# At the end of each stage: the second tile's scaled rows ahead of all splits

## The chip, the core and the metric

The kernel runs on one core of a Trainium2 chip. The core has five engines that this text calls PE (TensorE, the matrix multiplier), DVE (VectorE), ACT (ScalarE), POOL (GpSimd) and SP (SyncE, which here issues the loads from memory). The metric is the device time of one execution in microseconds (us), less being better.

## What is computed

Two blocks on a batch of 256 tokens of width 1024, all in fp32. Cut to the order of the stages:

```python
# first block, i = 0 (mLSTM) and i = 1 (sgu)
h = rmsnorm(x, norm_g[i, 0]) * (1.0 + sc1) + sh1       # sc, sh, g: rows of silu(c) @ ada_w[i] + ada_b[i]
y = mlstm_mixer(h, ...) if i == 0 else sgu_mixer(h, ...)
x = x + g1 * rmsnorm(y, norm_g[i, 1])
h = rmsnorm(x, norm_g[i, 2]) * (1.0 + sc2) + sh2
y = square(relu(h @ ffn_w1[i])) @ ffn_w2[i]
x = x + g2 * rmsnorm(y, norm_g[i, 3])
# second block
h = rms_norm(x, attn_norm_g); proj = h @ w_in          # attention and convolution branches, gated
x = x + mixed @ w_out
h2 = rms_norm(x, ffn_norm_g); x = x + peer(h2, ...)    # experts picked by product keys
h3 = rms_norm(x, ple_norm_g)
x = x + sigmoid(h3 @ w_ple_gate) * (p @ w_ple_proj)
```

Each stage ends in the same way: a residual add, a norm over 1024 columns, a scale (and a shift), and the next stage's first matrix product.

## The kernel before

The 256 tokens are two tiles of 128. An fp32 product is made of three products of split operands: `split` (L351) writes `hi`, the operand cast to a shorter form (ACT, L352), and `lo`, the rest (DVE, L353); PE then adds hi·hi, lo·hi and hi·lo (L113, or L384 to L386 for transposed results). Weights arrive as `st` tiles of 128x2048 fp32 (1 MB), loaded by SP in program order (L358) into a pool of three buffers, `wst`; each is split in two halves, `hi`/`lo` of 128x1024. A buffer is free for the next load when the last reader of its tile is done. A scheduler lays down one fixed order of instructions on each engine; `behind()` (L294) adds a constraint: what is issued inside it stands behind the instructions `net.lo` (DVE) and `net.hi` (ACT) on their engines. The weights' splits use it too (L372), each behind the one before it.

The end of a stage is `Finish`. `chain(t)` makes the norm of tile t and its normed rows `xn` (DVE L191, ACT L192). `turn(t)` transposes `xn` in eight 128x128 pieces on PE (L203), four into the PSUM tile `sd` and four into `mm`; DVE scales and shifts the first four (L212), ACT the other four (L214, or L216 with a shift), into `hf`. `split(t)` makes `hhi` (ACT) and `hlo` (DVE) of these rows. `run(t)` is the head: the next stage's first columns, computed by PE in plain fp32 (L135) from the unsplit weights and from `hf`, so that PE has work while the splits are made. The head's weights are two or three `st` tiles, held until tile 1's head has read them. There are seven such ends: into the mLSTM (1), the first ffn (2), the sgu (3), the second ffn (4), the mixing stage of the second block (5), the experts (6) and the last stage (7, which has no head). Text and rows below use these numbers. The tiles of the rows and of the order: `ada` is an accumulator of the modulation rows on DVE, fed by `ada_w` loads; `b_w_v` and `b_w_u` are the sgu's weights, `ffn_w2` the second ffn's, `peer_q` the experts' queries'.

`end` (L229 to L243) is the place of the change: behind the `xn` rows (`self.at`) it issues tile 0's splits, then tile 1's `turn`, `run` and splits.

Of the kernel before, what the change touches and what calls it, by code (L numbers as in the profile page):

```python
# [16 lines left out]
AF = mybir.ActivationFunctionType  # L17
ALU = mybir.AluOpType
# [119 lines left out]
class Finish:  # L138
# [55 lines left out]
    def turn(self, t):  # L194

        net, nc = self.net, self.net.nc
        g, sh = self.g, self.sh
        pss = []
        for q in range(2):
            ps = (net.sd_tile, net.mm_tile)[q]().rearrange("p (k c) -> p k c", k=4)  # L200
            for k in range(4):
                kk = 4 * q + k
                nc.tensor.transpose(ps[:, k], self.xn[:, kk * 128:(kk + 1) * 128], net.ident)  # L203
            pss.append(ps)
        for q, ps in enumerate(pss):
            hf = self.room(512, 1024 * t + 512 * q, "hf", 4).rearrange("p (k c) -> p k c", k=4)
            self.hf[t, q] = hf
            for k in range(4):
                kk = 4 * q + k
                gk, sk = g[:, kk:kk + 1], None if sh is None else sh[:, kk:kk + 1]  # L210
                if q == 0:
                    nc.vector.tensor_scalar(hf[:, k], ps[:, k], gk, sk, op0=ALU.mult, op1=ALU.bypass if sh is None else ALU.add)  # L212
                elif sh is None:
                    nc.scalar.activation(hf[:, k], ps[:, k], AF.Copy, scale=gk)  # L214
                else:
                    nc.scalar.activation(hf[:, k], ps[:, k], AF.Identity, scale=gk, bias=sk)  # L216

    def split(self, t):
        for q in range(2):
# [8 lines left out]
    def end(self, acc, last=None):  # L228

        net = self.net  # L230
        if self.head is not None:
            net.head = Head(net, self.head, self.head_pool)
        self.chain(1, acc)
        self.run(0)

        net.lo, net.hi = self.at
        with net.behind():
            if self.head is not None:
                self.x = net.h_tiles()
                self.split(0)  # L240
            self.turn(1)
            self.run(1)
            self.split(1)  # L243

    def whole(self):
# [17 lines left out]
class Net:  # L263
# [613 lines left out]
    def mix(self, x):  # L877
        nc, a = self.nc, self.a
        with ExitStack() as es:
# [168 lines left out]
            def head(h):  # L1048
                pl = self.sd_tile()[:, :384]
                for t, s, w in segs:  # L1050
                    nc.tensor.matmul(pl[:, s], qn[:, h // 2, t * 128:(t + 1) * 128], kz[:, h, :w], start=True, stop=True)
                lg = p2.tile([128, 384], F32, tag="rl", name="lg")
                nc.vector.tensor_tensor(lg, pl, bm[:, h], op=ALU.add)
                mx = self.small.tile([128, 2], F32, tag="mx", name="mx")
                pr = p2.tile([128, 384], F32, tag="pr", name="pr")
                for t, s, w in segs:
                    nc.vector.tensor_reduce(mx[:, t:t + 1], lg[:, s], axis=AX.X, op=ALU.max, negate=True)
                    nc.scalar.activation(pr[:, s], lg[:, s], AF.Exp, bias=mx[:, t:t + 1], accum_out=rs[:, t, h:h + 1])

                def turn():  # L1060
                    pt = self.sd_tile()[:, :384]
                    for e in range(3):
                        b = slice(e * 128, (e + 1) * 128)
                        nc.tensor.transpose(pt[:, b], pr[:, b], self.ident)
                    pts = p2.tile([128, 384], F32, tag="pts", name="pts")
                    self.last = nc.scalar.copy(pts, pt)
                    self.defer(lambda: weigh(pts))

                def weigh(pts):
                    vs = slice(h * 64, (h + 1) * 64)  # L1070
                    nc.tensor.matmul(av[1][:, vs], pts[:, 0:128], v[:, 0, vs], start=True, stop=False)
                    nc.tensor.matmul(av[1][:, vs], pts[:, 128:256], v[:, 1, vs], start=False, stop=True)
                    nc.tensor.matmul(av[0][:, vs], pts[:, 256:384], v[:, 0, vs], start=True, stop=True)

                self.defer(turn)
# [432 lines left out]
```

## Time and profile before

| what | us |
|---|---|
| median of three runs (lowest, highest) | 1772.01 (1771.02, 1776.46) |
| the profiled execution | 1775.46 |
| its span from the first to the last instruction | 1773.8 |
| PE busy | 1719.7 (97%) |
| DVE busy | 1385.0 (78%) |
| ACT busy | 873.9 (49%) |

Each row of the timeline is an instruction, or several of one kind in a row (x4): its start, how long the group took, engine, line, what it writes and reads, and in brackets how long the engine had been idle before and what ended that. The mean granted clock of PE over the span was 0.994 of full speed.

### The profile page before, as it was taken

Reading aid. Unit: us, or ns where it says so; the run is one execution under the profiler, and the core shown is the slowest. Engines: PE = TensorE matmul, PEld = TensorE weight load, DVE = VectorE, ACT = ScalarE, POOL = GpSimd, SP = SyncE. Lnnn points to the kernel's source line nnn. Section 1 sums busy time; section 2 is a strip of 40 time slices with the busy share of each in tenths; the row PEclk is TensorE's granted clock in tenths of the full one; section 3 lists DMA queues with packets and bytes.
Section 4 is the critical chain, followed back from the end, with each engine's and each line's share of the span. In section 5 each row is a group of like instructions: output and inputs, shape, how many; then the busy total and the mean of one; then the engine's idle time right before and its main releaser. Section 6 shows DMA issues by size and latency. Waiting matters only on the chain.

```text
span 1773.8 us, 29281 instructions
## 1 busy us (share of the span) xinstructions
PE 1719.7 (97%) x11754; PEld 1537.7 (87%) x11754; DVE 1385.0 (78%) x2394; ACT 873.9 (49%) x1404; POOL 27.6 (2%) x42
## 2 busy tenths in 40 slices
PE   7998999999999999999899999999999999999998
PEld 3877899987889898889889999999988998787786
DVE  6687986578958555899757999789788948888754
ACT  3564555454545444565545445445444444455544
POOL 0010000000000000000000000000000000000000
PEclk9999999999999999999899999999999999999999
DMA  9875987376838552544426555544555455554751
GB/s 334 299 286 186 335 354 257 138 270 243 303 118 294 186 190 95 198 143 143 146 95 219 183 174 183 182 166 168 175 176 180 144 190 175 182 186 155 258 190 48
DMA packets 59603, 352.48 MB, mean 199 GB/s; under 512 B 6165, under 2 KB 12613, under 8 KB 19273
## 3 DMA queue, kind: packets, MB, share of 16 engines
q1 hardware_dynamic: 59466, 350.61, 56.3%
q8 instruction: 92, 1.51, 0.3%
q14 instruction: 45, 0.37, 0.1%
HBM read 349.51 MB, written 1.07 MB: 198 GB/s over the span
## 4 chain that ended last, share of the span: by engine, by line
PE 83%; DVE 8%; DMA 3%; ACT 3%; issue 2%; POOL 1%; SPq 0%; POOLq 0%; DVEq 0%; ACTq 0%
PE acc L113 37%; PE mm L384 13%; PE mm L386 13%; PE mm L385 13%; DVE lo L353 2%; PE head L135 2%; PE sd L1171 1%; PE sd L1182 1%; ACT hi L352 1%; DVE ada L509 1%; ACT junk L164 1%; DMA st<-in_a_w_v_dram 1%; PE sd L804 1%; DMA X<-in_x_dram 1%; POOL rs_r L429 0%
## 5 line engine op out<-in xcount | busy, mean ns | idle before, releaser
L352 ACT CAST hi<-st 128x1024 fp32r<-128x1024 f32 (+1 forms) x507 | 525.7, 1048 | 487.6 <-PE mm L385 234.8
L353 DVE TENSOR_TENSOR lo<-st,hi 128x1024 fp32r<-128x1024 f32 (+1 forms) x507 | 613.9, 1220 | 174.5 <-ACT hi L352 172.9
L384 PE MATMUL mm<-hhi,hi 128*128 128x256 f32 (+1 forms) x2000 | 574.0, 287 | 1.9 <-ACT hi L352 1.2
L386 PE MATMUL mm<-hhi,lo 128*128 128x256 f32 (+1 forms) x2000 | 566.5, 284 | 4.9 <-DVE lo L353 4.8
L385 PE MATMUL mm<-hlo,hi 128*128 128x256 f32 (+1 forms) x2000 | 566.7, 283 | 0.0
L386 PEld LDWEIGHTS mm<-hhi,lo 128*128 128x128 f32 (+1 forms) x2000 | 383.2, 192 | 5.8 <-DVE lo L353 5.7
L384 PEld LDWEIGHTS mm<-hhi,hi 128*128 128x128 f32 (+1 forms) x2000 | 383.5, 192 | 4.5 <-ACT hi L352 1.8
L385 PEld LDWEIGHTS mm<-hlo,hi 128*128 128x128 f32 (+1 forms) x2000 | 383.6, 192 | 2.2 <-issue 1.1
L113 PE MATMUL acc<-hi,vh 128*128 128x512 f32 x448 | 142.5, 399 | 0.9 <-ACT vh L352 0.9
L113 PE MATMUL acc<-lo,vh 128*128 128x512 f32 x448 | 138.8, 391 | 0.0
L113 PE MATMUL acc<-hi,vl 128*128 128x512 f32 x448 | 137.9, 389 | 0.0
L113 PE MATMUL acc<-hi,h 128*128 128x512 f32 x320 | 100.7, 394 | 0.0
L113 PEld LDWEIGHTS acc<-hi,vl 128*128 128x128 f32 x448 | 84.1, 188 | 18.4
L113 PEld LDWEIGHTS acc<-lo,vh 128*128 128x128 f32 x448 | 84.1, 188 | 18.1
L113 PE MATMUL acc<-lo,h 128*128 128x512 f32 x320 | 99.3, 390 | 0.1
L113 PE MATMUL acc<-hi,l 128*128 128x512 f32 x320 | 99.1, 390 | 0.0
L509 DVE SCALAR_TENSOR_TENSOR ada<-st,cact,ada 128x1024 f32<-128x1024 f32 x74 | 94.6, 1279 | 5.5 <-DMA st<-in_ada_w_dram 5.0
L113 PEld LDWEIGHTS acc<-hi,vh 128*128 128x128 f32 x448 | 80.5, 188 | 15.1 <-ACT vh L352 1.3
L352 ACT CAST vh<-gx 128x512 fp32r<-128x512 f32 x64 | 39.9, 625 | 83.0 <-PE acc L113 80.8
L1161 DVE TENSOR_TENSOR A<-iota,rT 128x1024 f16<-128x1024 f16 x96 | 66.1, 689 | 16.5 <-PE sd L1171 16.5
L113 PE MATMUL acc<-hi,hhi 128*128 128x512 f32 x224 | 72.4, 403 | 4.7 <-ACT hi L352 3.0
L113 PE MATMUL acc<-lo,hhi 128*128 128x512 f32 x224 | 73.1, 400 | 0.1
(396 smaller groups left out, 2176.7 us busy)
## 6 DMA issues: line engine op xcount, KB each, us to landing
st<-in_peer_u_dram SPq DMA_DIRECT2D x64, 1024.0 KB, 4.8
st<-in_peer_v_dram SPq DMA_DIRECT2D x64, 1024.0 KB, 4.9
st<-in_ffn_w_dram SPq DMA_DIRECT2D x63, 1024.0 KB, 4.9
st<-in_ada_w_dram SPq DMA_DIRECT2D x40, 1024.0 KB, 5.2
st<-in_ada_w_dram SPq DMA_DIRECT2D x16, 512.0 KB, 7.2
st<-in_b_w_u_dram SPq DMA_DIRECT2D x8, 1024.0 KB, 4.8
st<-in_b_w_v_dram SPq DMA_DIRECT2D x8, 1024.0 KB, 5.5
st<-in_b_w_out_dram SPq DMA_DIRECT2D x8, 1024.0 KB, 5.2
```

The lines of the kernel that those rows point to most:

```text
L113: ins = mm(self.t[t][j], a[:, ts], b[:, j * 512:(j + 1) * 512], start=first and a is xh and b is wh, stop=last and a is xl)
L135: net.nc.tensor.matmul(ps[:, t * 128:(t + 1) * 128], w[:, k], x(k), start=k == 0, stop=k == KD - 1)
L164: nc.scalar.activation(net.junk[:, halves[h]], src, AF.Square, scale=1.0 / 32.0, accum_out=out[:, h:h + 1])
L352: i = self.nc.scalar.copy(hi, src)
L353: return i.ins, self.nc.vector.tensor_tensor(lo, src, hi.bitcast(F32), op=ALU.subtract).ins
L384: mm(out, ahi, bhi, start=start, stop=False)
L385: mm(out, ahi, blo, start=False, stop=False)
L386: return mm(out, alo, bhi, start=False, stop=stop)
L509: nc.vector.scalar_tensor_tensor(s, w, c, s, op0=ALU.mult, op1=ALU.add)
L804: nc.tensor.matmul(ps[:, t], v[:, t, n * 128:(n + 1) * 128], ws[:, n], start=False, stop=t == 1)
L1161: nc.vector.tensor_tensor(A, iota2.unsqueeze(1).to_broadcast([128, 4, 128, 2]), pairs(iT, 128), op=ALU.is_equal)
L1171: nc.tensor.matmul(pg[:, i], A[:, i // 2, :, i % 2], B[:, :, i // 2, :, i % 2], start=True, stop=True)
```

## The change

The order inside `end`: `turn(1)` comes first, and returns its last row on each engine; tile 1's head follows; both tiles' splits and all later splits of weights stand behind those last rows, not behind the `xn` rows. For stage 7 only `split(1)` is left behind them. Lines after the change are two higher from L218 on.

```diff
         for q, ps in enumerate(pss):
...
                 if q == 0:
-                    nc.vector.tensor_scalar(hf[:, k], ps[:, k], gk, sk, op0=ALU.mult, op1=ALU.bypass if sh is None else ALU.add)
+                    lo = nc.vector.tensor_scalar(hf[:, k], ps[:, k], gk, sk, op0=ALU.mult, op1=ALU.bypass if sh is None else ALU.add)
                 elif sh is None:
-                    nc.scalar.activation(hf[:, k], ps[:, k], AF.Copy, scale=gk)
+                    hi = nc.scalar.activation(hf[:, k], ps[:, k], AF.Copy, scale=gk)
                 else:
-                    nc.scalar.activation(hf[:, k], ps[:, k], AF.Identity, scale=gk, bias=sk)
+                    hi = nc.scalar.activation(hf[:, k], ps[:, k], AF.Identity, scale=gk, bias=sk)
+        return lo.ins, hi.ins
...
         net.lo, net.hi = self.at
         with net.behind():
+            net.lo, net.hi = self.turn(1)
+        self.run(1)
+        with net.behind():
             if self.head is not None:
                 self.x = net.h_tiles()
                 self.split(0)
-            self.turn(1)
-            self.run(1)
             self.split(1)
```

The number of instructions of every engine stays the same. How the order moves is shown at three places; the numbers behind names tell buffers and tiles apart, and `waits` names the semaphores that an instruction waits on.

ACT at the end of stage 2 (`hf` rows L216 of tile 1, `hhi` of both tiles, `hi` of the ffn's first weights), before:

```order
L352 CAST hhi_1408<-hf_1332 128x4x128
L352 CAST hhi_1408<-hf_1337 128x4x128
L352 CAST hi_1524<-st_1522 128x1024 [waits DMAHW3_49]
L352 CAST hi_1528<-st_1522 128x1024
L216 ACTIVATE hf_1429<-mm_1419,sh2_0_106,sc2_0_107 128x128 [waits PE_49]
L216 ACTIVATE hf_1429<-mm_1419,sh2_0_106,sc2_0_107 128x128 x3
L352 CAST hhi_1408<-hf_1429 128x4x128 [waits Activation_49]
L352 CAST hhi_1408<-hf_1424 128x4x128 [waits DVE_49]
```

and after:

```order
L216 ACTIVATE hf_1423<-mm_1413,sh2_0_106,sc2_0_107 128x128 [waits PE_49]
L216 ACTIVATE hf_1423<-mm_1413,sh2_0_106,sc2_0_107 128x128 x3
L354 CAST hhi_1460<-hf_1332 128x4x128
L354 CAST hhi_1460<-hf_1337 128x4x128
L354 CAST hhi_1460<-hf_1418 128x4x128 [waits DVE_49]
L354 CAST hhi_1460<-hf_1423 128x4x128 [waits Activation_49]
L354 CAST hi_1524<-st_1522 128x1024 [waits DMAHW3_49]
L570 ACTIVATE r_1490<-head_1374 128x256 [waits PE_49]
L354 CAST hi_1528<-st_1522 128x1024
```

The four rows L216 stand right behind `xn`, and the two casts of weights behind all four `hhi`.

DVE at the end of stage 3 (`lo_3416` and `lo_3420` split the load of `b_w_v` that is there already, `lo_3459` and `lo_3463` the next one, `st_3456`), before:

```order
L353 TENSOR_TENSOR hlo_3336<-st_2981,hhi_3335 128x4x128 [waits Activation_49] x2
L353 TENSOR_TENSOR lo_3416<-st_3413,hi_3415 128x1024 [waits DMAHW5_49,Activation_49]
L212 TENSOR_SCALAR st_2981<-sd_3341,sc1_1_1472,sh1_1_1471 128x128 [waits PE_49]
L212 TENSOR_SCALAR st_2981<-sd_3341,sc1_1_1472,sh1_1_1471 128x128 x3
L353 TENSOR_TENSOR lo_3420<-st_3413,hi_3419 128x1024 [waits Activation_49]
L353 TENSOR_TENSOR hlo_3336<-st_2981,hhi_3335 128x4x128 [waits Activation_49] x2
L500 MEMSET ada_3449 128x1024
L509 SCALAR_TENSOR_TENSOR ada_3449<-st_3452,cact_96,ada_3449 128x1024 [waits DMAHW7_49,DMAHW6_49,DVE_49]
L509 SCALAR_TENSOR_TENSOR ada_3449<-st_3452,cact_96,ada_3449 128x1024 [waits DVE_49]
L353 TENSOR_TENSOR lo_3459<-st_3456,hi_3458 128x1024 [waits DMAHW0_49,Activation_49]
L353 TENSOR_TENSOR lo_3463<-st_3456,hi_3462 128x1024 [waits Activation_49]
L509 SCALAR_TENSOR_TENSOR ada_3449<-st_3490,cact_96,ada_3449 128x1024 [waits DMAHW1_49,DVE_49]
```

and after:

```order
L212 TENSOR_SCALAR st_2981<-sd_3335,sc1_1_1472,sh1_1_1471 128x128 [waits PE_49]
L212 TENSOR_SCALAR st_2981<-sd_3335,sc1_1_1472,sh1_1_1471 128x128 x3
L355 TENSOR_TENSOR hlo_3386<-st_2981,hhi_3385 128x4x128 [waits Activation_49] x4
L355 TENSOR_TENSOR lo_3416<-st_3413,hi_3415 128x1024 [waits DMAHW5_49,Activation_49]
L355 TENSOR_TENSOR lo_3420<-st_3413,hi_3419 128x1024 [waits Activation_49]
L502 MEMSET ada_3449 128x1024
L355 TENSOR_TENSOR lo_3459<-st_3456,hi_3458 128x1024 [waits DMAHW7_49,Activation_49]
L511 SCALAR_TENSOR_TENSOR ada_3449<-st_3452,cact_96,ada_3449 128x1024 [waits DMAHW6_49,DMAHW0_49,DVE_49]
L355 TENSOR_TENSOR lo_3463<-st_3456,hi_3462 128x1024 [waits Activation_49]
L511 SCALAR_TENSOR_TENSOR ada_3449<-st_3452,cact_96,ada_3449 128x1024 [waits DVE_49]
L511 SCALAR_TENSOR_TENSOR ada_3449<-st_3490,cact_96,ada_3449 128x1024 [waits DMAHW1_49,DVE_49]
L511 SCALAR_TENSOR_TENSOR ada_3449<-st_3490,cact_96,ada_3449 128x1024 [waits DVE_49]
```

The rows L212 moved ahead of four `hlo`; `lo_3459` moved ahead of both additions of `st_3452` to `ada`, and `lo_3463` ahead of the second.

SP at the same place, before:

```order
L358 DMA st_3452<-in_ada_w_dram 128x2048 [waits DMAHW5_49,DVE_49]
L501 DMA ada_3449<-in_ada_b_dram 1x1024 [waits DMAHW7_49,DVE_49,PE_49]
L358 DMA st_3456<-in_b_w_v_dram 128x2048 [waits DMAHW3_49,PE_49]
L358 DMA st_3490<-in_ada_w_dram 128x2048 [waits DMAHW4_49,PE_49]
L358 DMA st_3494<-in_b_w_v_dram 128x2048 [waits DMAHW6_49,DVE_49]
L358 DMA st_3504<-in_ada_w_dram 128x2048 [waits DMAHW0_49,DVE_49]
L358 DMA st_3508<-in_b_w_v_dram 128x2048 [waits DMAHW1_49,DVE_49]
```

and after:

```order
L360 DMA st_3452<-in_ada_w_dram 128x2048 [waits DMAHW3_49,PE_49]
L360 DMA st_3456<-in_b_w_v_dram 128x2048 [waits DMAHW5_49,DVE_49]
L503 DMA ada_3449<-in_ada_b_dram 1x1024 [waits DVE_49]
L360 DMA st_3490<-in_ada_w_dram 128x2048 [waits DMAHW4_49,PE_49]
L360 DMA st_3494<-in_b_w_v_dram 128x2048 [waits DMAHW7_49,DVE_49]
L360 DMA st_3504<-in_ada_w_dram 128x2048 [waits DMAHW6_49,DVE_49]
L360 DMA st_3508<-in_b_w_v_dram 128x2048 [waits DMAHW1_49,DVE_49]
```

The first `ada_w` load now takes a buffer that PE frees; `st_3456` waits for DVE; `st_3494` now takes the buffer of `st_3456`, where it took that of `st_3452`.

## Rows read from the trace of the kernel before

**Rows 1.** The page's first part, busy time, share and instructions of each engine:

```profile
PE 1719.7 (97%) x11754; PEld 1537.7 (87%) x11754; DVE 1385.0 (78%) x2394; ACT 873.9 (49%) x1404; POOL 27.6 (2%) x42
```

**Rows 2.** PE's waits over the span: total us, times, longest:

```profile
PE mm L384 <- ACT cTh L352: 5.4, 1, 5.4
...
PE head L135 <- DVE hf L212: 4.1, 3, 2.3
...
PE head L135 <- DVE st L212: 2.1, 2, 1.2
...
PE head L135 <- DVE v L212: 1.2, 1, 1.2
```

**Rows 3.** Timeline, end of stage 2, tile 0: transposes and the rows behind them:

```profile
159.69 0.60 PE L203 MATMUL mm<-kc,xn 128*128 128x128 f32 x4
...
160.33 1.51 ACT L216 ACTIVATE hf<-mm,sh,sc 128x128 f32<-128x128 f32 x4 [0.97 <-PE mm L203]
```

**Rows 4.** Timeline, end of stage 2, tile 1, up to the head's first result:

```profile
168.20 0.60 PE L203 MATMUL sd<-kc,xn 128*128 128x128 f32 x4
...
168.64 0.60 PE L203 MATMUL mm<-kc,xn 128*128 128x128 f32 x4
...
170.74 1.49 ACT L216 ACTIVATE hf<-mm,sh,sc 128x128 f32<-128x128 f32 x4
171.06 1.36 DVE L212 TENSOR_SCALAR hf<-sd,sc,sh 128x128 f32<-128x128 f32 x4
171.53 5.18 PE L135 MATMUL head<-hf,st 128*128 128x128 f32 x44 [2.29 <-DVE hf L212]
...
176.07 0.39 ACT L568 ACTIVATE r<-head 128x256 f32<-128x256 f32 x1 [2.66 <-PE head L135]
```

**Rows 5.** Timeline of SP, after the end of stage 3: issues of loads:

```profile
366.20 0.34 SPq L358 DMA_DIRECT2D st<-in_b_w_v_dram  x1
...
370.96 0.33 SPq L358 DMA_DIRECT2D st<-in_b_w_v_dram  x1
...
376.97 0.33 SPq L358 DMA_DIRECT2D st<-in_b_w_v_dram  x1
```

**Rows 6.** Timeline of ACT and of DVE, same stretch: splits, and additions to `ada`:

```profile
362.22 1.14 ACT L352 CAST hhi<-st 128x512 fp32r<-128x512 f32 x2
...
370.98 2.00 ACT L352 CAST hi<-st 128x1024 fp32r<-128x1024 f32 x2 [0.48 <-DMA st<-in_b_w_v_dram]
377.10 2.00 ACT L352 CAST hi<-st 128x1024 fp32r<-128x1024 f32 x2 [4.12 <-DMA st<-in_b_w_v_dram]
...
368.32 2.60 DVE L509 SCALAR_TENSOR_TENSOR ada<-st,cact,ada 128x1024 f32<-128x1024 f32 x2 [2.53 <-DMA st<-in_ada_w_dram]
372.06 2.36 DVE L353 TENSOR_TENSOR lo<-st,hi 128x1024 fp32r<-128x1024 f32 x2 [1.13 <-ACT hi L352]
...
384.31 2.36 DVE L353 TENSOR_TENSOR lo<-st,hi 128x1024 fp32r<-128x1024 f32 x2 [0.92 <-ACT hi L352]
```

**Rows 7.** Timeline, end of stage 4 and the first use of `ffn_w2`:

```profile
523.88 5.62 PE L135 MATMUL head<-v,st 128*128 128x128 f32 x48 [1.24 <-DVE v L212]
...
525.94 12.03 SPq L358 DMA_DIRECT2D st<-in_ffn_w_dram  x5
...
533.54 0.73 PE L113 MATMUL acc<-lo,h 128*128 128x512 f32 x2
```

**Rows 8.** Timeline, end of stage 6, first use of the next `peer_q`; then stage 7:

```profile
926.78 6.27 SPq L358 DMA_DIRECT2D st<-in_w_peer_q_dram  x3
927.07 5.62 PE L135 MATMUL head<-hf,st 128*128 128x128 f32 x48 [0.95 <-DVE hf L212]
...
936.21 0.36 PE L384 MATMUL mm<-hhi,hi 128*128 128x256 f32 x1
...
1750.43 1.12 ACT L214 ACTIVATE gxr<-mm,cols 128x128 f32<-128x128 f32 x4
```

**Rows 9.** Table by stretch, behind PE's idle of 5.4 us; PEclk is third from the end:

```profile
880.00:885.00 5.00, 3.78 (x16) 3.49 (x17) 2.19 (x3) 0.00 (x0) 0.00 (x0) 0.50 0.62 213
```

## The prediction

> **What bounds the kernel now.** Read first the busy shares: PE is busy in 97% of the span [rows 1], so a change can gain only where PE stands idle, and costs wherever it makes PE wait anew. Then read PE's waits over the whole span, to see what is on offer. The head's waits for the scaled rows L212 are 4.1 + 2.1 + 1.2 = 7.4 us in all, over the six stage ends that have a head [rows 2]. This is the whole prize: 0.42% of the time. Third, read the stage ends one by one, to see what stands ahead of those rows: at the end of stage 2 the transposes of tile 1 start at 168.20 and 168.64, but the rows only at 171.06 on DVE and 170.74 on ACT, behind splits [rows 4]. For tile 0, with nothing in between, ACT's rows start 0.64 us after their transposes (160.33 against 159.69) [rows 3]. Last, read what follows the head: stage 3 lives on loads, and there ACT stands idle for 4.12 us until one lands [rows 6].
>
> **Gain at the rows.** Stage 2: by the 0.64 us of tile 0 the rows start at 168.84 on DVE and at 169.28 on ACT. The head's first column needs all eight rows in order. Today the last to come is DVE's fourth, at 171.06 + 1.36 = 172.42; five products of 5.18 / 44 = 0.12 us are then left, end 173.0 [rows 4]. After, the last is ACT's fourth, at 169.28 + 1.5 = 170.8, with one product left, end 170.9. So the head ends **2.1 us** earlier, nearly all of the 2.29 us that PE idles there. The same arithmetic in the others takes most of their share of the 7.4 us, in all some 6 us, since ACT's rows, not DVE's, become the last. Nothing is removed: the splits and casts that stood ahead of the rows stand behind them now, and they are needed too, by the next products and, above all, by the loads.
>
> **Who pays: the loads.** A buffer of `wst` is freed by its last reader. In the order before, the first load behind a stage end waits for a `lo` on DVE. In the order after, it takes the buffer that PE's head frees, and the delayed `lo` frees the next. The head is done with its first weights 4.5 us after its start (176.07 - 171.53) [rows 4].
> Stage 2: the head now starts at 169.3, so its buffer is free at about 173.8 to 174.1, against 172.42 + 1.2 = 173.6 today, when DVE has made the `lo` behind its rows [rows 4, 6]. I see no new wait of PE behind that, and keep **-2.1**; bounds -2.3 (the whole idle) and -1.0 (half lost to DVE, which has the same splits to do later).
> Stage 3: the chain is DVE's. `lo_3420` now stands behind four `hhi` and two `hi` of ACT. Today ACT is done with casts and rows at 362.22 + 1.14 = 363.4 [rows 6]; after, it idles between `xn` and the rows for two groups of transposes and the 0.64 behind them, some 1.6 to 1.9, and is done at 365.0 to 365.3, `lo_3420` 1.2 later and a little of DVE's own queue, 366.5 to 366.8; the load of `st_3456` goes out there, against 366.20 [rows 5], and beside another load it lands near 371.4, against 370.9. Now the order on DVE counts. Before, the two additions of `st_3452` stand ahead of `lo_3459`, at 368.32, and fill DVE's wait [rows 6]; after, they stand behind it. And `st_3494` no longer takes the buffer of `st_3452`, free at 370.9, but that of `st_3456`, free when `lo_3463` ends: `hi` ends at 372.5, then `lo` 1.2, addition 1.3, `lo` 1.2 make 376.2. The load goes out at 376.2 against 370.96, lands at 381 to 382 against 377.10, and PE, with 24 products of a load to do, stands idle for about 4 us. DVE does its two additions more in the meantime; the load of `st_3508` goes out at 376.2 + 3 x 1.3 = 380.1 against 376.97, and its `lo` starts at about 387.7 against 384.31. From there I take it that DVE, busy without a pause, hands the delay on to PE. So **+3.3**; bounds +2 (additions of later loads fill in, as they do today) and +4.6 (PE's stall is passed on whole).
> Stage 4: the head starts 1.2 us earlier, at 522.7, and frees its first buffer at 527.2 to 527.5; today this load goes out at 525.94 [rows 7]. Landing 4.8 (370.98 - 366.20 [rows 5, 6]) + `hi` 1.0 + `lo` 1.2 gives 534.2 to 534.5 for the product that starts at 533.54 today [rows 7]: the gain of 1.2 is gone, and **+0.9** comes; bounds -0.9 and +1.2.
> Stage 6: the head starts 0.9 earlier, at 926.1, and frees its buffer at 930.6; today the load goes out at 926.78, ahead of the head's start [rows 8]. 930.6 + 4.8 + 1.0 = 936.4 for `hi`, 937.6 for `lo`, where the first product with them runs at 936.21 and needs `lo` 0.3 later: **+1.1**; bounds -0.8 and +2 (DVE's search of the top scores now stands ahead of that `lo`).
> Stage 5 is of the same kind, but PE has other products to bring forward, and DVE starts its long convolution earlier: I take **0**, between the gain of 1.2 there [rows 2] and stage 4's loss, 0.9. Stage 1: the head runs on without a pause there and the rows keep their place, 0; at best the 0.9 that is left of rows 2. Stage 7 has no head; ACT's rows at 1750.43 [rows 8] come earlier, but PE waits for `hhi` and one `lo` that now come later: **+0.4**, between -0.3 and +1.2 (one `lo`).
> Sum: -2.1 + 3.3 + 0.9 + 0 + 1.1 + 0 + 0.4 = **+3.6 us**. On the profiled execution, 1775.46 (1773.8 of span and 1.7 around it), this is 1779.1; that execution lies 3.5 us above the median of the three runs, and the forecast stands on the median: 1772.0 + 3.6 = **1775.6**.
>
> **Rivals.** *A: the gain is kept.* The loads that go out later were early enough, and DVE's additions in stage 3 find another gap. Then 6 us of the 7.4 remain: **1766**. For it: in stage 2 nothing waits behind the head. The Trainium skill (Trainium Kernel Development and Optimization, Best Practices) says to double-buffer so that loads overlap with compute; by that rule three buffers hide a load that goes out some us later, and the time would be A's. Against it: in stage 3 three buffers do not hide the loads even now, with 4.12 us of ACT's idle until one lands [rows 6].
> *B, slower: PE's new stall in stage 3 halves its clock.* Behind PE's idle of 5.4 us elsewhere in this trace [rows 2] the granted clock is 0.50, and the 16 products there take 3.78 us, twice the 0.12 us of each at full clock [rows 9, 4]. If the 4 us at `hi` of `st_3494` do the same, the products behind them take about 4 us more for 4 us of work at half speed, of which some 1.7 is on the chain, since DVE is late as well; stage 3 then costs 5.0, and with the upper ends of stages 4 and 6 the sum is -2.1 + 5.0 + 1.2 + 2.0 + 0.5 + 0.4 = +7.0: **1779**. It decides from the point where PE's idle in one piece nears that 5.4 us; the head's 2.29 us of today are followed by products at full speed [rows 4]. The Trainium skill (TensorE: Matmul & The Clock Gate, Part 1) says that the throttled clock is the default and activity releases it; the trace agrees at 880 us [rows 9], and by that rule a long stall costs more than its length, as B has it.
> *C: nothing changes.* What PE gains at each head it gives back at the first split behind it, no more and no less: **1772**. For it: the same splits have to be made by the same engines. Against it: stage 2 has nothing to give back to, stage 3 loses by buffers, not by splits.
>
> **How the numbers follow.** The sum's own case 0.43, its range 1773 to 1778; A 0.20; B 0.27; C 0.10. A measurement of this kernel can tell about 0.3%, 5.3 us, from no change. A is 6 us faster, so three quarters of it, 0.15, count as faster by more than that; B, with a small upper tail of the sum, as slower, 0.31; the rest, 0.54, is within it. The range goes from A's 1766 to B's 1779 and 1 us beyond, for the bound of 4.6 in stage 3.
>
> **What would show it.** In the profile after: PE's head at stage 2 waiting under 0.4 us, and each stage's first load released by PE; in stage 3 a wait of PE of about 4 us for `hi` of `b_w_v` near 378, and the end of the sgu some 3 us later against its start; a wait of 0.5 to 2 us for `lo` or `hi` at the first product of `ffn_w2` and of `peer_q`. Wrong would be: no such wait in stage 3, or DVE without idle there; then A is right. A granted clock under 0.8 in the stretch after that stall speaks for B.

## The result, and the profile after

The changed kernel takes 1783.67 us (median of five runs, 1782.36 to 1787.47) against 1772.01 us: a ratio of 1.0065, with a 95% interval from 1.0047 to 1.0082. It is slower by 11.7 us. The forecast was 3.6 us slower, with a range that ended at 1780. Its profiled execution has a span of 1781.6 us, 7.8 more than the one of before. Of all executions that this text counts, one is an outlier: of the six of the kernel with early rows and early loads (below), one took 7376.51 us, the other five 1762.76 to 1765.63, and its ratio is of those five.

What the change was made for does happen. The timeline of the end of stage 2 (start, length, engine, line, what it writes and reads, idle before): the rows follow the transposes, and the head follows the rows:

```profile
167.11 0.60 PE L203 MATMUL sd<-kc,xn 128*128 128x128 f32 x4
167.55 0.60 PE L203 MATMUL mm<-kc,xn 128*128 128x128 f32 x4
167.75 1.37 DVE L212 TENSOR_SCALAR hf<-sd,sc,sh 128x128 f32<-128x128 f32 x4 [1.16 <-PE sd L203]
168.19 1.51 ACT L216 ACTIVATE hf<-mm,sh,sc 128x128 f32<-128x128 f32 x4 [1.36 <-PE mm L203]
168.22 5.96 PE L135 MATMUL head<-hf,st 128*128 128x128 f32 x51
```

The 2.29 us of [rows 4] are gone, and none of the waits of [rows 2] for rows of stages 2 to 6 is left. PE's waits from 345 to 960 us (total us, times, longest) show what stands in their place:

```profile
PE acc L113 <- ACT hi L354: 6.2, 4, 3.4
...
PE mm L386 <- ACT hi L354: 2.7, 3, 1.8
PE sd L869 <- issue: 1.2, 1, 1.2
```

The first two lines are waits for casts of weights, that is for loads. The third is at stage 5, and the profile doesn't show what it waits for; the product there reads `rb`, whose load goes out between the two late loads of `w_qi`. In stage 3 the issues on SP answer to [rows 5]:

```profile
363.18 0.33 SPq L360 DMA_DIRECT2D st<-in_b_w_v_dram  x1
...
373.17 0.33 SPq L360 DMA_DIRECT2D st<-in_b_w_v_dram  x1
...
377.01 0.33 SPq L360 DMA_DIRECT2D st<-in_b_w_v_dram  x1
```

The `xn` rows at this stage's end start 3.27 us earlier than before (353.88 against 357.15), so on the old clock the second and third loads went out at 376.4 and 380.3, against 370.96 and 376.97. DVE's timeline shows why: it stands idle 5.36 us at the `lo` that now precedes the additions to `ada`, and then does work that before had filled the wait [rows 6]:

```profile
369.59 1.23 DVE L355 TENSOR_TENSOR lo<-st,hi 128x1024 fp32r<-128x1024 f32 x1 [5.36 <-ACT hi L354]
370.73 1.28 DVE L511 SCALAR_TENSOR_TENSOR ada<-st,cact,ada 128x1024 f32<-128x1024 f32 x1
371.93 1.22 DVE L355 TENSOR_TENSOR lo<-st,hi 128x1024 fp32r<-128x1024 f32 x1
373.06 3.92 DVE L511 SCALAR_TENSOR_TENSOR ada<-st,cact,ada 128x1024 f32<-128x1024 f32 x3
379.06 2.36 DVE L355 TENSOR_TENSOR lo<-st,hi 128x1024 fp32r<-128x1024 f32 x2 [2.08 <-ACT hi L354]
```

PE's timeline at the same place: an idle of 3.38 us, and behind it products that take twice as long as ahead of it (two in 1.22 or 1.05 us, where two took 0.61):

```profile
375.09 0.61 PE L113 MATMUL acc<-hi,hlo 128*128 128x512 f32 x2
379.08 1.22 PE L113 MATMUL acc<-hi,hhi 128*128 128x512 f32 x2 [3.38 <-ACT hi L354]
380.34 1.22 PE L113 MATMUL acc<-lo,hhi 128*128 128x512 f32 x2
381.36 1.05 PE L113 MATMUL acc<-hi,hlo 128*128 128x512 f32 x2
```

Stage 4 shows the same with a shorter idle; the load goes out at 528.18, against 525.94 [rows 7]:

```profile
534.17 1.20 PE L113 MATMUL acc<-hi,h 128*128 128x512 f32 x4 [1.84 <-ACT hi L354]
535.43 1.22 PE L113 MATMUL acc<-lo,h 128*128 128x512 f32 x2
536.45 1.05 PE L113 MATMUL acc<-hi,l 128*128 128x512 f32 x2
...
539.34 0.62 PE L113 MATMUL acc<-lo,h 128*128 128x512 f32 x2
```

The table by stretch (busy time of PE, its weight loads, DVE, ACT, POOL; then the granted clock, DMA share and GB/s) has the clock well under 1 behind each of the four stage ends 3 to 6; 0.5 is the lower of its two levels, 1.2 of 2.4 GHz:

```profile
375.00:380.00 5.00, 1.62 (x6) 0.74 (x4) 2.88 (x3) 1.99 (x2) 0.00 (x0) 0.83 0.94 383
380.00:385.00 5.00, 4.96 (x12) 3.69 (x12) 4.00 (x4) 0.82 (x1) 0.00 (x0) 0.50 0.98 357
...
535.00:540.00 5.00, 4.94 (x15) 3.66 (x14) 4.28 (x6) 3.53 (x5) 0.00 (x0) 0.66 0.88 313
725.00:730.00 5.00, 3.68 (x17) 3.28 (x18) 5.00 (x8) 2.76 (x3) 0.00 (x0) 0.64 0.42 117
730.00:735.00 5.00, 5.00 (x32) 5.00 (x32) 3.10 (x6) 0.37 (x1) 0.00 (x0) 0.67 0.86 291
...
945.00:950.00 5.00, 4.84 (x29) 4.74 (x29) 5.00 (x16) 2.37 (x3) 0.00 (x0) 0.67 0.59 188
```

The same table of the kernel before has 1.00 at the same place of each of the four stages (in stages 5 and 6 from 720 to 730 and from 935 to 945); of stages 3 and 4:

```profile
380.00:385.00 5.00, 5.00 (x24) 4.14 (x23) 3.81 (x4) 1.77 (x2) 0.00 (x0) 1.00 0.97 338
...
535.00:540.00 5.00, 5.00 (x31) 4.42 (x29) 4.97 (x5) 3.71 (x5) 0.00 (x0) 1.00 0.86 287
```

Where the 7.8 us between the two spans came from is read off the start of `xn` of tile 1 at each stage end, after against before: -1.1 at stage 2, -3.3 at 3, +0.9 at 4, +3.4 at 5, +6.3 at 6, +7.5 at 7. From one end to the next that is -2.2, +4.2, +2.5, +2.8, +1.3, and +0.3 to the end. Such differences are of two single executions: the part from the end of stage 1 to that of stage 2, where the order hardly changes, differs by 1.8 us too. The profiles of the runs below help, since each keeps the old order at most ends. In the old order, the part from the end of stage 3 to that of stage 4 takes 162.5 to 162.9 us in six of them, and 163.8 in the profile of before; after the change it takes 168.0. So +4.2 is too little there, and +5.1 to +5.5 nearer. From stage 4 to 5 the old order takes 188.3 us in all six that have it unchanged, before included, so +2.5 stands.

### The profile page after: what moved, and what is told of

It reads as the page before. It is cut to its first block, busy times and chain, and to the rows that moved or that the text cites. A ratio compares the mean times of both kernels' runs of the same rounds, so it can differ in the third digit from the quotient of the medians.

```text
span 1781.6 us, 29286 instructions
## 1 busy us (share of the span) xinstructions
PE 1728.1 (97%) x11754; PEld 1543.7 (87%) x11754; DVE 1386.8 (78%) x2394; ACT 873.8 (49%) x1404; POOL 28.0 (2%) x42
## 4 chain that ended last, share of the span: by engine, by line
PE 86%; DVE 7%; DMA 2%; ACT 2%; issue 1%; POOL 1%; SPq 0%; POOLq 0%; DVEq 0%; ACTq 0%
PE acc L113 38%; PE mm L386 13%; PE mm L388 13%; PE mm L387 13%; PE head L135 3%; DVE lo L355 2%; PE sd L1173 1%; PE sd L1184 1%; DVE ada L511 1%; DMA st<-in_ada_w_dram 1%; PE sd L485 1%; ACT hi L354 1%; DMA st<-in_b_w_v_dram 1%; DMA st<-in_a_w_v_dram 1%; DVE yc L899 1%
```

## The experiments

The theories. **L**: the loads behind a stage end go out later, and that is the cost, with PE's low clock behind the stalls. **S**: the splits of the tiles, now behind the rows, are themselves what PE waits for next, at every end. **R** (in one run): the early rows do harm. **G** (in the expectations): the loss belongs to no single end. The time of each run stands against runs of the kernel before on the same chip.

**The new order at one end alone.** `end` counts its calls, and takes the new order at one number (2 in the first kernel, then 3, 4, 5 and 6; there are only seven ends, so 9 never comes) and the old one, which is left out below, at the others:

```diff
         net.lo, net.hi = self.at
+        net.ends = getattr(net, "ends", 0) + 1
+        if net.ends in (2, 9):
             with net.behind():
                 net.lo, net.hi = self.turn(1)
             self.run(1)
...
```

Stage 2:

> The new order at the end of stage 2 alone, the old one at the other six ends. Theory L (the loss comes from loads that go out later, where loads are what the stage lives on): PE's head starts 2.2 us earlier, no load is late enough to matter, so -2.0 to -2.2 us against before, about 1770. Rival S (the splits that now stand behind the rows are themselves what PE waits for next, at every end): the 2 us are given back at the first split product, 0 to +2 us. Rival G (the loss isn't local to any stage end): no change.

1769.35 us against 1772.33, ratio 0.9979 (0.9970 to 0.9989): 3 us faster. L's sign and, within the interval, its size; S falls here.

Stage 3:

> The new order at the end of stage 3 alone. Theory L: the second load of b_w_v takes a buffer that comes free 5 us later, PE stands idle 3 to 4 us there, and its clock is low behind it: +3.5 to +4.5 us against before. Rival S: +1 to +2 us, as at any other end, without an idle of PE of over 2 us. Rival G: no change.

1777.59 against 1772.33, ratio 1.0029 (1.0015 to 1.0043): 5.3 us slower, with an idle of PE of 3.4 us at the cast of `b_w_v`.

Stage 4:

> The new order at the end of stage 4 alone. Theory L: the first load of ffn_w2 goes out some 1.3 us later against the old schedule and 2.2 later against PE's own, PE idles 1.8 us for its cast and runs at a low clock behind that: +2 to +3 us. Without the clock's part it would be +0.9. Rival S: +1 to +2. Rival G: no change.

1775.81 against 1772.33, ratio 1.0018 (1.0009 to 1.0028): 3.5 us slower. PE's timeline there, and the table by stretch:

```profile
529.59 1.54 PE L113 MATMUL acc<-hi,h 128*128 128x512 f32 x4 [1.85 <-ACT hi L364]
...
531.86 1.05 PE L113 MATMUL acc<-hi,l 128*128 128x512 f32 x2
```

```profile
530.00:535.00 5.00, 5.00 (x16) 3.68 (x15) 4.54 (x5) 3.77 (x5) 0.00 (x0) 0.66 0.87 324
```

Stage 5:

> The new order at the end of stage 5 alone. Theory L: the first load of the query indexer's weights goes out later, PE waits for its split, and its clock falls behind that: +2 to +3.5 us. The prediction's term was 0. Rival S: +1 to +2. Rival G: no change.

1777.57 against 1772.33, ratio 1.0035 (1.0022 to 1.0048): 5.2 us slower, more than L said. PE waits there 1.2, 0.9 and 0.4 us in place of the head's 1.2 and one wait of 1.0, hardly more in all, but the clock is 0.66 from 720 to 725; in the profiled execution the stage costs 1.9 us. That execution is the fastest of the seven, 1773.54 us, 4 us under their median; what the rest of the 5.2 is, its trace can't show.

Stage 6:

> The new order at the end of stage 6 alone. Theory L: the first load of the next peer_q goes out 3.7 us later, PE waits 1.8 us for its cast and 0.6 for the next two, at a low clock behind that: +1 to +3 us against before. Rival S: +1 to +2. Rival G (not local): no change.

1776.98 against 1773.34, ratio 1.0017 (1.0006 to 1.0028): 3.6 us slower; PE waits 1.8 us at the cast of `peer_q`, and the clock is 0.66 behind it.

The cost is local to the ends, so G falls: four ends lose and one gains. The five add up to -3.0 + 5.3 + 3.5 + 5.2 + 3.6 = 14.6 us, against 11.7 for the whole change, which is as close as intervals of 2 us each allow. Stages 1 and 7 were not run alone.

**The load late, the rows as before.** In stage 4 alone of the old order, the weights' parts are put behind the tiles' splits (`tail` is the last split of tile 1):

```diff
                 self.turn(1)
                 self.run(1)
                 self.split(1)
+            if net.ends == 4:
+                net.hi, net.lo = self.tail
```

> The kernel before with one thing moved, at the end of stage 4 alone: the weights' parts stand behind all splits of both tiles; the second tile's rows keep their old place. The head starts as before, only lo of the weights at hand ends some 2.4 us later and with it the first load of ffn_w2 goes out at about 528.4 instead of 525.9. Theory L (the late load is the cost): PE waits about 2 us at the first product of ffn_w2, and with the low clock behind that +2 to +3.5 us against before. Rival R (the rows' early place is what harms): no change.

1777.77 against 1773.19, ratio 1.0029 (1.0018 to 1.0040): 4.6 us slower, without a row moved. R falls, and L's cause is there alone. The head starts 1.2 us before its old time, as everything up to there, and the load only 0.5 us later by the clock, so 1.7 us later against the head:

```profile
526.48 11.48 SPq L372 DMA_DIRECT2D st<-in_ffn_w_dram  x5
```

```profile
532.66 1.20 PE L113 MATMUL acc<-hi,h 128*128 128x512 f32 x4 [1.47 <-ACT hi L366]
533.92 0.73 PE L113 MATMUL acc<-lo,h 128*128 128x512 f32 x2
534.48 0.62 PE L113 MATMUL acc<-hi,l 128*128 128x512 f32 x2
```

In this execution the clock stayed up behind the 1.47 us, and the stage costs 1.5 us; the median of the timed runs lies 3 us higher. Its mean granted clock over the span is 0.994, as before; the six other executions have 0.991 or 0.992.

**The rows early, the loads early.** Rows first and the tiles' splits behind them, as in the change; but the weights' `hi` may stand ahead of the rows on ACT, in its gap behind `xn`, and their `lo` right behind the rows on DVE:

```diff
         with net.behind():
-            net.lo, net.hi = self.turn(1)
+            rows = self.turn(1)
         self.run(1)
+        at = rows[0], net.hi
+        net.lo, net.hi = rows
         with net.behind():
             if self.head is not None:
                 self.x = net.h_tiles()
                 self.split(0)
             self.split(1)
+        net.lo, net.hi = at
```

> At every stage end the second tile's rows still come first, and both tiles' splits still follow them, but the weights' parts do not follow the splits: on ACT the casts stand in the gap between xn and the rows, on DVE the lo stands right behind the rows, ahead of hlo. So the loads' buffers come free as early as in the old order or earlier. Theory L (late loads cost the time): the gain at the heads stays, -5 to -7 us against before, no wait of PE over 1 us at the first load of stages 3, 4 and 6. Rival S (the late splits of the tiles cost the time): as slow as the changed kernel, +5 to +12 us.

1764.41 against 1773.34, ratio 0.9943 (0.9926 to 0.9961): **9 us faster than the kernel before**, and some 19 faster than the changed one. S falls: the tiles' splits are as late as in the change. The timeline of stage 3's end, where ACT casts between `xn` and the rows, and DVE makes the first `lo` behind the rows and ahead of `hlo`:

```profile
352.23 1.98 ACT L357 CAST hi<-st 128x1024 fp32r<-128x1024 f32 x2
...
353.53 1.37 DVE L212 TENSOR_SCALAR st<-sd,sc,sh 128x128 f32<-128x128 f32 x4 [1.45 <-PE sd L203]
354.00 7.41 PE L135 MATMUL head<-st 128*128 128x128 f32 x64
354.11 1.49 ACT L216 ACTIVATE st<-mm,sh,sc 128x128 f32<-128x128 f32 x4
354.82 1.22 DVE L358 TENSOR_TENSOR lo<-st,hi 128x1024 fp32r<-128x1024 f32 x1
...
356.14 2.50 DVE L358 TENSOR_TENSOR hlo<-st,hhi 128x512 fp32r<-128x512 f32 x4
```

The loads of `b_w_v` behind it, 5.55 us earlier than before by `xn` (351.60 against 357.15): 366.8, 371.6 and 377.8 on the old clock, against 366.20, 370.96 and 376.97 [rows 5], so still 0.6 to 0.9 late, where the change had the second 5.5 late:

```profile
361.22 0.34 SPq L363 DMA_DIRECT2D st<-in_b_w_v_dram  x1
...
366.06 0.33 SPq L363 DMA_DIRECT2D st<-in_b_w_v_dram  x1
...
372.29 0.33 SPq L363 DMA_DIRECT2D st<-in_b_w_v_dram  x1
```

PE's longest wait for a cast of weights on its accumulators in stages 3 to 6 is now 0.9 us, where it was 3.4:

```profile
PE acc L113 <- ACT hi L357: 1.9, 3, 0.9
```

Not every stage gains. In the profile, the part from the end of stage 3 to that of stage 4 takes 165.4 us, against 163.8 before and 162.5 to 162.9 in six other profiles with the old order: there this kernel still loses, and it gains behind the ends of stages 2, 4, 5 and 6.

The forecast for it was 5 to 7 us. The clock may be the rest: a head's wait, too, costs more than its length in some executions, and this kernel has none behind stage 1. Eight profiles have the old order at the end of stage 2, each with the head's wait of 2.29 us. In six the clock stayed up, and 189.9 to 190.0 us pass to the end of stage 3; in two it fell (in that of the late load and that of stage 5 alone), and 191.6 pass. Of these eight, that of stage 6 alone and that of the late load:

```profile
170.00:175.00 5.00, 5.00 (x47) 5.00 (x47) 2.84 (x5) 1.84 (x5) 0.00 (x0) 1.00 0.52 185
170.00:175.00 5.00, 5.00 (x32) 5.00 (x32) 2.83 (x5) 1.44 (x3) 0.00 (x0) 0.67 0.45 146
```

So the same idle in the same order costs 1.6 us more when the clock falls. At the end of stage 5, behind the head's wait of 1.2 us, it fell in three of eight profiles with the old order; in the run with stage 2 alone it is 0.66 from 710 to 715.

**The same with the weights' `lo` ahead of the rows:**

```diff
-        at = rows[0], net.hi
+        at = net.lo, net.hi
```

> As the kernel before, with tile 0's splits moved behind the second tile's rows, and the weights' parts ahead of the rows on both engines (in the gap between xn and the rows, and past it). The loads go out as early as before, the rows start about as late as before (DVE does one or two lo first). Theory L: within 2 us of before, since neither the heads nor the loads move by much. Rival S: the tiles' splits are as late as in the changed kernel, so +5 us or more.

1774.23 against 1773.34, ratio 1.0008 (0.9997 to 1.0019): no change that could be told, as L said; S, which said 5 us or more, falls here too. The gain of the previous kernel hangs on `lo` standing behind the rows.

**Useless work in PE's idle.** Two kernels take the new order at one end alone and add transposes into a tile that nobody reads, behind the head, 20 for stage 3 and 16 for stage 4. For stage 3:

```diff
             self.run(1)
+            for _ in range(5):
+                ps = net.sd_tile().rearrange("p (k c) -> p k c", k=4)
+                for k in range(4):
+                    net.nc.tensor.transpose(ps[:, k], self.xn[:, k * 128:(k + 1) * 128], net.ident)
```

> The new order at the end of stage 3 alone, with 20 more transposes on PE behind the head there, whose results nobody reads (2.3 us of added PE work). DVE's and SP's order is that of the run with stage 3 alone. If half the cost there comes from PE's low clock behind its idle of 3.4 us: the idle shrinks to about 1.2 us, the granted clock stays near 1.0, and the kernel is 0.5 to 2 us faster than stage 3 alone in spite of the added work. If the load's lateness alone is the cost: the same time as stage 3 alone, within 0.5 us. If PE's work were the bound there: 2 us slower.

1775.55 against 1773.34, ratio 1.0012 (1.0002 to 1.0023), against 1.0029 (1.0015 to 1.0043) without them. Inconclusive as to the clock, since the added work was too short: an idle of 1.86 us was left, with half speed behind it:

```profile
381.43 1.78 PE L113 MATMUL acc<-hi,hhi 128*128 128x512 f32 x4 [1.86 <-ACT hi L368]
383.00 1.05 PE L113 MATMUL acc<-lo,hhi 128*128 128x512 f32 x2
```

It does show that PE's work is not what bounds stage 3 there: with 2.3 us more of it the stage takes as long as without (3.1 us more than before in both profiles).

For stage 4:

> The new order at the end of stage 4 alone, with 16 more transposes on PE behind the head there, whose results nobody reads (1.8 us, as long as PE's idle for ffn_w2's first cast was). If the clock is half of the cost there: PE's idle is gone, the granted clock stays at 1.0, and stage 4 costs about 1.0 us against before instead of the 2.3 to 2.5 us seen, 1 to 1.5 us less than without the added work. If the clock has no part: 2.3 to 2.5 us as without.

1773.26 against 1773.19, ratio 1.0006 (0.9997 to 1.0015), against 1.0018 (1.0009 to 1.0028) without the added 1.8 us of work. In the profiles the stage costs 0.7 us instead of 2.3. No idle is left, and the clock stays at 1.00 where it was 0.66:

```profile
531.07 1.20 PE L113 MATMUL acc<-hi,h 128*128 128x512 f32 x4
532.33 0.73 PE L113 MATMUL acc<-lo,h 128*128 128x512 f32 x2
532.91 0.62 PE L113 MATMUL acc<-hi,l 128*128 128x512 f32 x2
```

```profile
530.00:535.00 5.00, 4.83 (x25) 3.65 (x24) 3.07 (x4) 3.70 (x6) 0.00 (x0) 1.00 0.98 382
535.00:540.00 5.00, 5.00 (x36) 4.65 (x35) 3.98 (x5) 3.05 (x4) 0.00 (x0) 1.00 0.86 300
```

Part of ACT's and DVE's order moved too (the first two casts of weights now stand ahead of one `r` and one `h`), and PE's first product of `ffn_w2` starts 12.0 us behind the stage's `xn` instead of 12.3. So of the 1.6 us, 0.3 are this earlier start; the other 1.3 of stage 4's 2.3 us are the clock, in an idle that could be filled at no cost. The timed executions agree. Their mean granted clock gives the time at the low level (the share that is missing from 1, doubled, times the span): 27.5 us on average with stage 4 alone, 22.9 us with the added work, and 22.7 us in the kernel before.

## Why the prediction was wrong

The sign was right, and so were the late loads and the places where PE waits for them. What failed is the price of such a wait: the sum charged its length, and left the low clock behind it to rival B, for one long idle in stage 3 only. Step by step:

- **Gain at the rows.** -2.1 for stage 2; -2.2 in the profiles, 3 us in the timed run with that end alone. Right.
- **Loads in stage 3.** The two loads were put at 376.2 and 380.1; they went out at 376.4 and 380.3 on the old clock. The term was +3.3, the profile has +4.2 (5.1 to 5.5 against the other profiles), the run with that end alone 5.3; B had 5.0. The working of the loads holds; what it lacked is the products at half speed behind the idle.
- **Stage 4.** The term was +0.9. In the profile PE's products of `ffn_w2` start 1.0 us later, against `xn`, than before: the step was right. Then eight products at half speed add 1.5, and the stage costs 2.5, outside the bound of 1.2. The run with added work, in a kernel with that end alone, takes 1.3 such us away.
- **Stage 5.** The term was 0. PE's new waits are 1.2 + 0.45 + 0.87 = 2.5 us, in place of the head's 1.2 and one of 1.0 for a `lo`: by waits alone +0.3, and the term holds. But behind them lie the longest stretch at the low clock, 0.64 and 0.67 over ten us, and the stage costs +2.8 in the profile, 5.2 in the timed run: 2.5 us are products at half speed.
- **Stage 6.** +1.1; the profile has +1.3, the run with that end alone +3.6 and 3.2 in its profile. The part behind this end is 825 us long and takes 822.5 to 825.8 in eight profiles with the old order, so the profiles can't size the term; the timed run says that it was too small, and the clock of 0.67 behind the wait is the likely reason.
- **Stage 7**: +0.4, and 0.3 in the profile, no more than profiles with the old order differ there (25.7 to 26.3 us).
- **The step that failed for the sum: rival B's condition.** B had the mechanism, but for one place, and "from the point where PE's idle in one piece nears that 5.4 us". Idles of 1.8 us, and several short ones in a row, were followed by the low level at all four ends of the profiled execution. The timed executions show the same: by their mean granted clock (0.988 after, 0.9936 in 73 executions of the kernel before), PE is at the low level for 41.4 us on average, against 22.7. Work that takes 18.7 us at half speed takes half of that at full speed, so up to 9.3 us of the loss are the clock. At 1.5 to 2.5 us in each of the four places the sum of +3.6 would have been +9.6 to +13.6; 11.7 was measured. The trace of before had the warning: behind an idle of 2.07 us at 74 us its table by stretch has 0.66, a row that I left out for the head's 2.29 us at stage 2, behind which the clock stayed up in that execution. Two such rows with opposite outcomes should have made a term with a chance of its own at each new stall, and a range that reaches beyond 1780:

```profile
75.00:80.00 5.00, 4.94 (x15) 3.62 (x14) 4.71 (x5) 1.88 (x3) 0.00 (x0) 0.66 0.87 315
```

- **The rivals.** A and C fall with the single ends: stages 3 to 6 lose each by itself. The Trainium skill's rule that A was weighed with (Trainium Kernel Development and Optimization, Best Practices, on overlapping loads and compute) does not hold at these ends, by PE's waits of 3.38 and 1.84 us for loads that go out later. B's low clock is in the runs, with 0.66 in stage 4 and 1.00 where the idle is filled with work. The Trainium skill (TensorE: Matmul & The Clock Gate, Part 1) has activity release the throttle; those two rows agree.

What stays open: how much of each single end's cost is the clock. The timed runs with one end alone cost 0.4 to 3.3 us more than their own profiles show in that stage. These profiles are not of typical executions: that of before is 3 us above its kernel's median, those of stages 3 and 5 alone are 3 and 4 us below theirs, and the clock falls in some executions and not in others behind the same idle. The kernel with early loads gains 9 us and not 6; it is at the low level for 16.2 us on average, 6.5 less than before, which is worth up to 3.2 us. That would close the gap, but these means are of the whole span, and don't tell at which end the time was lost.

## What to carry to other kernels

When instructions are moved ahead on an engine, ask what they were moved past: here the casts and subtractions of weights, whose real product is a free buffer, and a load behind it. Put what frees a buffer right behind the urgent work and ahead of what is needed only some us later, and most of the gain is kept (9 us here, where the plain swap lost 12). And price every new stall of PE at its length and, as a second term with its own chance, some products at half speed behind it.

## What was not expected of the hardware

- PE's granted clock was at 0.66 over the 5 us behind idles of 1.84 and 1.85 us, and 0.50 behind 3.38 us; behind 1.47 us (the late load) it stayed at 1.00. The same idle of the same order can do either: behind 2.29 us at stage 2 it fell in two profiles of eight, and behind 1.2 us at stage 5 in three of eight. At stage 2 the fall cost 1.6 us.
- Work without use in an idle of PE made the changed stage faster than without it: 1.8 us of transposes took stage 4 from +2.3 to +0.7 us, 1.3 of it by the clock.
